# Modulation steps by single halves over all tiles, an unscaled residual stream, and a head-by-head split in a two-layer hybrid decoder

## The chip, the cores and the metric

The kernel runs on one core of a Trainium2 chip. The metric is the device time of one execution in microseconds; the median of the runs shown counts, and beside it one execution was profiled. TensorE is the matrix engine (PE in the profile), VectorE is DVE, ScalarE is ACT, GpSimd is POOL, and SyncE (SP) issues all DMA transfers.

## The reference

Two layers over 256 tokens of width 2048, float32. `shift`, `scale` and `gate` come from one conditioning vector per sequence; making them is what is called the modulation here.

```python
def hybrid_layer(x, c_act, positions, ada_w, ada_b, norm_w, w_in, ...):
    mod = c_act @ ada_w + ada_b
    shift, scale, gate = mod[:, :D_MODEL], mod[:, D_MODEL:2 * D_MODEL], mod[:, 2 * D_MODEL:]
    h = rmsnorm(x, norm_w) * (1.0 + scale[:, None, :]) + shift[:, None, :]
    u = h @ w_in
    qkv_a, beta_a, a_a, z_a, q_b, k_b, v_b, z_b, g_a, g_b = split_cols(u, SPLIT_SIZES)
    ...
    # branch A: causal conv and SiLU on q, k, v; normed q, k; gated delta rule in chunks
    o_a = gated_delta_rule(q_a, k_a, v_a, g, beta)
    o_a = rmsnorm(o_a, gdn_norm_w).reshape(b, s, GDN_WIDTH).astype(x.dtype) * jax.nn.silu(z_a)
    # branch B: rotary positions, sliding-window attention with sinks
    o_b = swa_with_sinks(q_b, k_b, v_b, sinks).reshape(b, s, SWA_WIDTH) * jax.nn.silu(z_b)
    y = jax.nn.sigmoid(g_a) * (o_a @ proj_a) + jax.nn.sigmoid(g_b) * (o_b @ proj_b)
    return x + gate[:, None, :] * (y @ w_out)
```

After both layers a final RMSNorm is applied. The modulation needs 3 x 16 column blocks of 128 in each layer, each the product of a 128x2048 block of `ada_w` with the activated conditioning vector.

## The kernel before

Everything is held transposed: 128 channels on the partitions, the 256 tokens along the row. A projection tile is one 128-column block of a weight matrix, 128x2048 floats. `load_w` (L205) fetches it as two halves of 128x1024 into the buffer `win` (five of these). `load_half` (L196) splits each half into a rounded part `whi`, cast by ScalarE (L201), and the residue `wlo`, subtracted by VectorE (L202); there are four `whi` and three `wlo` buffers. `proj` (L292) makes 16 steps of contraction, each one matmul of `whi` with 512 columns (the rounded part and the residue of the activations side by side, L289) and one of `wlo` with 256 (L290). Two PSUM banks take turns as accumulators. `evac` (L314) empties one: a copy by ScalarE (L316) and an addition by VectorE (L317), result `ub`.

The main loop (L967 to L1001) goes through the tiles of `_plan` (L46): the short ones (ba, kb, vb), then for each of two batches of eight heads qa, ka, va and, between them, the queries and gates of branch B (qb, zb); then za (the gates of branch A), pa, pb (the two output projections) and wo. Layer 0 makes the merge gates ga and gb in a group ahead of the loop; layer 1 makes eight ga tiles so and has the others within the loop, alternating with pa and pb. At a tile the loop issues the loads up to two tiles ahead, the matmuls, one step of each waiting stream (`advance`, L303), one step of the background queue (`run_bg`, L956), and then the tile's handler. The functions are traced by a framework that derives all semaphores from the tiles and sets the order on each engine from priority (program order) and readiness, so that an engine's order can depart from that of the text. On the chip each engine works through its list strictly in that order.

Three things go on beside the projections:

- *The modulation.* `ada_job` (L171) makes one column block: `ada_half` (L165) loads a 128x1024 half of `ada_w` into one of the five `win` buffers and multiplies it on VectorE with the conditioning vector, summing along the row (L168); two halves in succession, then one or two tiny operations (L177, L180). 64 such jobs are on the list (L423): the 16 gates of layer 0, then scale, shift and gate of layer 1. `ADA_RATE` (L28) gives how many jobs a tile of each kind is worth, and L993 to L996 issue a job whenever the sum reaches one. 48 must be done before layer 0's wo; the last 16 follow in layer 1's ga, pa, gb and pb tiles.
- *The preparation of branch A* (`gdn_k`, L589, and `gdn_core`, L729), a generator in the background queue, one step per tile between `yield`s: norms (`brk`, L596), a transpose on TensorE and a broadcast through DRAM (L598), decay tables, Gram matrices (L623, L624), the inversion of 32x32 triangular blocks on VectorE (L644 to L653), small DMAs that turn the blocks round (L658 to L670), matmuls that join them (T1p at L679 and following), then the chunk recurrence, whose output is `oT`. Batch 0's generator starts at va 0, batch 1's at va 8. `gdn_e` (L556) makes the decay tables `E` and `ek` of a batch when its first qa tile is handled.
- *The outputs.* `h_za` (L778) multiplies each head of `oT` with its weight and gate (L785). After every eighth za tile `split_oA` (L788) casts and subtracts two groups of four heads (L321, L322) into `oA_hl`, which pa multiplies. `split_oB` (L888) does the same for branch B at pa 2.

In wo, `h_wo` (L928) adds the gated tile to the residual (L936, L937), adds its square to the norm's sum (`norm_acc`, L358), and in layer 0 writes `x` to DRAM (L942), scales it in place by layer 1's scale (L943) and forms the two parts of `raw` (L951, L952), with which layer 1's first gates are begun before its norm is known (`group_next`, L266). `h_step` (L376) then makes layer 1's normed `h` from the scaled `x`.

## Time and profile before

| what | value |
|---|---|
| median of 3 runs | 2373.2 us (2370.95 to 2382.15) |
| the profiled execution | 2373.67 us, of which the span is 2371.9 us |
| ScalarE's share of the span | 58% |
| DMA | 531.76 MB, mean 224 GB/s |
| layer 0's loop begins, ends | 216.35, 1223.3 us |
| layer 1's loop begins | 1276.21 us |

The span runs from the first to the last instruction. A line of a group reads: line in the code, engine, operation, result <- operands, shapes, count; then busy time and the mean of one in ns; then the time that the engine stood idle in front of them, and what ended it. A line of waits reads: who <- whom, total us, times, longest. Stages are told apart by the first matmul that uses their tile.

### The profile page before, as it was taken

The numbers are of one execution on the slowest core, as the hardware profiler recorded it, in microseconds if no ns is written. First come the engines' busy times: TensorE is split into PE (matmuls) and PEld (weight loads), VectorE is DVE, ScalarE is ACT, GpSimd is POOL, SyncE is SP. The second block draws the span as 40 slices with busy tenths as digits, with TensorE's granted clock in tenths as the row PEclk, the third lists the DMA queues.
The fourth block names the chain that finished last, engine by engine and source line by source line (L and its number), as shares of the span: only waits on it lengthen the run. The fifth ranks groups of instructions, "written<-read, shape, count | busy, mean of one in ns | idle before, by whom it ended". The sixth has DMA issues, their size and how long they took to land.

```text
span 2371.9 us, 40130 instructions
## 1 busy us (share of the span) xinstructions
PE 2294.8 (97%) x15094; PEld 2026.0 (85%) x15094; DVE 1791.0 (76%) x3176; ACT 1372.8 (58%) x2621; POOL 13.9 (1%) x20
## 2 busy tenths in 40 slices
PE   7999999999999998999999999999999999999997
PEld 6999888788887887888789888888888888888886
DVE  8997888867888577788676778757786567667766
ACT  4436566667666664444445665777667755444543
POOL 0000000000000000000000000000000000000000
PEclk9999999999999999999999999999999999999999
DMA  9998675656766577998666555535555467777764
GB/s 378 360 359 277 228 243 193 194 182 203 248 202 200 164 231 257 306 316 295 216 198 198 193 179 188 184 121 193 188 172 167 135 206 267 247 243 241 252 201 143
DMA packets 185604, 531.76 MB, mean 224 GB/s; under 512 B 40449, under 2 KB 69697, under 8 KB 179905
## 3 DMA queue, kind: packets, MB, share of 16 engines
q1 hardware_dynamic: 185410, 529.20, 67.1%
q8 instruction: 118, 1.93, 0.3%
q14 instruction: 76, 0.62, 0.1%
HBM read 512.26 MB, written 16.88 MB: 223 GB/s over the span
## 4 chain that ended last, share of the span: by engine, by line
PE 76%; DVE 11%; DMA 8%; issue 3%; ACT 2%; DVEq 0%; SPq 0%; ACTq 0%
PE mm L289 39%; PE mm L290 20%; DVE wlo L202 4%; DMA adaw<-ada 4%; PE mmg L251 2%; PE mmg L250 2%; PE mmg L249 2%; DMA win<-w 2%; DMA xs_dram<-x 1%; DVE adaw L168 1%; PE o L742 1%; PE ptr L872 1%; DVE cv L526 1%; PE sc L844 1%; PE mmg L273 1%
## 5 line engine op out<-in xcount | busy, mean ns | idle before, releaser
L289 PE MATMUL mm<-h,whi 128*128 128x512 f32 x3616 | 1294.8, 398 | 18.4 <-DVE ub L317 17.3
L202 DVE TENSOR_TENSOR wlo<-win,whi 128x1024 fp32r<-128x1024 f32 x724 | 882.5, 1221 | 253.0 <-PE mm L290 142.8
L290 PE MATMUL mm<-h,wlo 128*128 128x256 f32 x3616 | 1025.7, 284 | 3.8 <-DVE wlo L202 3.8
L201 ACT CAST whi<-win 128x1024 fp32r<-128x1024 f32 x724 | 754.8, 1048 | 461.9 <-PE mm L289 248.8
L289 PEld LDWEIGHTS mm<-h,whi 128*128 128x128 f32 x3616 | 682.5, 189 | 179.8 <-issue 10.6
L290 PEld LDWEIGHTS mm<-h,wlo 128*128 128x128 f32 x3616 | 683.5, 189 | 6.4 <-DVE wlo L202 5.1
L168 DVE SCALAR_TENSOR_TENSOR adaw<-adaw,cact 128x1024 f32<-128x1024 f32 x128 | 155.9, 1222 | 71.4 <-DMA adaw<-ada 70.1
L289 PE MATMUL mm<-yhl,whi 128*128 128x512 f32 x512 | 182.9, 398 | 7.6 <-DVE x L937 4.6
L289 PE MATMUL mm<-oAhl,whi 128*128 128x512 f32 x512 | 183.7, 400 | 5.4 <-DVE oAhl L322 3.3
L289 PE MATMUL mm<-oBhl,whi 128*128 128x512 f32 x512 | 180.8, 396 | 0.5 <-DVE ub L317 0.5
L317 DVE TENSOR_TENSOR ub<-ub,mm 128x256 f32<-128x256 f32 x290 | 120.8, 417 | 63.8 <-ACT ub L316 62.7
L526 DVE SCALAR_TENSOR_TENSOR cv<-ub,par,cv 128x255 f32<-128x255 f32 (+2 forms) x288 | 138.2, 480 | 34.1 <-ACT cv L524 30.4
L290 PE MATMUL mm<-oAhl,wlo 128*128 128x256 f32 x512 | 145.6, 285 | 1.1 <-DVE wlo L202 1.1
L249 PE MATMUL mmg<-h,whi 128*128 128x256 f32 x512 | 139.1, 286 | 6.5 <-ACT h L373 6.1
L290 PE MATMUL mm<-yhl,wlo 128*128 128x256 f32 x512 | 144.9, 283 | 0.0
L290 PE MATMUL mm<-oBhl,wlo 128*128 128x256 f32 x512 | 144.0, 281 | 0.0
L250 PE MATMUL mmg<-h,whi 128*128 128x256 f32 x512 | 141.0, 283 | 0.1
L251 PE MATMUL mmg<-h,wlo 128*128 128x256 f32 x512 | 134.1, 284 | 3.2 <-DVE wlo L202 3.2
L316 ACT COPY ub<-mm 128x256 f32<-128x256 f32 x290 | 107.2, 370 | 36.6 <-PE mm L290 36.4
L289 PEld LDWEIGHTS mm<-yhl,whi 128*128 128x128 f32 x512 | 96.8, 189 | 33.1 <-issue 7.2
L289 PEld LDWEIGHTS mm<-oAhl,whi 128*128 128x128 f32 x512 | 97.6, 191 | 29.4 <-DVE oAhl L322 3.6
L289 PEld LDWEIGHTS mm<-oBhl,whi 128*128 128x128 f32 x512 | 96.2, 188 | 23.7 <-DVE ub L317 0.9
(261 smaller groups left out, 2603.5 us busy)
## 6 DMA issues: line engine op xcount, KB each, us to landing
win<-w SPq DMA_DIRECT2D x724, 512.0 KB, 4.8
adaw<-ada SPq DMA_DIRECT2D x128, 512.0 KB, 4.8
adab<-ada SPq DMA_DIRECT2D x31, 1024.0 KB, 9.1
sg<-sig_dram SPq DMA_DIRECT2D x40, 128.0 KB, 5.6
sig_dram<-gacc SPq DMA_DIRECT2D x4, 1024.0 KB, 5.6
E<-gc_dram SPq DMA_DIRECT2D x4, 1024.0 KB, 7.2
GT<-GT_d SPq DMA_DIRECT2D x4, 1024.0 KB
ob_dram<-zbs SPq DMA_DIRECT2D x32, 128.0 KB, 4.7
```

The costliest lines, as they stand in the source:

```text
L168: V.scalar_tensor_tensor(t, t, 1.0, cact[:, hf * 1024:(hf + 1) * 1024], op0=ALU.mult, op1=ALU.mult, accum_out=acc[:, hf:hf + 1])
L201: A.copy(h, w)
L202: V.tensor_tensor(o, w, h.bitcast(F32), op=ALU.subtract)
L249: T.matmul(d, hi, m[:, 0:S], start=(k == b0 and t % 2 == 0), stop=False)
L250: T.matmul(d, hi, m[:, S:2 * S], start=False, stop=False)
L251: T.matmul(d, lo, m[:, 0:S], start=False, stop=(k == b1 - 1 and t % 2 == 1))
L273: T.matmul(d, hi[:, c], m[:, 0:n], start=(k == 0), stop=False)
L289: T.matmul(ps[:, :], hi[k // 8][:, c0:c0 + P], m, start=(k == 0), stop=False)
L290: T.matmul(ps[:, S:2 * S], lo[k // 8][:, c0:c0 + P], m[:, 0:S], start=False, stop=(k == KT - 1))
L316: A.copy(t, ps[:, S:2 * S])
L317: V.tensor_tensor(t, t, ps[:, 0:S], op=ALU.add)
L526: V.scalar_tensor_tensor(y[:, j:], u[:, :S - j], w(3 - j), y[:, j:], op0=ALU.mult, op1=ALU.add)
```

## The change

Four edits go together.

1. The modulation is issued in half steps (`ada_step`): each step loads and multiplies one half; the second of a block also does the tiny operations. The list holds 128 half steps, and the sum of rates counts twice. The rates of layer 0 are new: qa and ka lower, va no longer zero, qb, zb and za higher, pa and pb lower. Layer 1's stay.
2. `x` isn't scaled in place any more. `raw` is made with the scale as an operand, and so is `h_step`'s product.
3. `split_oA` is gone. `h_za` casts and subtracts its own head right after the multiplication.
4. `gdn_k` has one empty step more after `brk` and one more before T1p.

```diff
-ADA_RATE = [dict(qa=0.45, ka=0.45, va=0.0, qb=0.275, zb=0.275, za=0.54, pa=0.54, pb=0.54), dict(ga=0.3, pa=0.3, gb=0.3, pb=0.3)]
+ADA_RATE = [dict(qa=0.25, ka=0.25, va=0.15, qb=0.45, zb=0.45, za=0.6, pa=0.45, pb=0.45), dict(ga=0.3, pa=0.3, gb=0.3, pb=0.3)]
...
-        def ada_job(l, part, ct):
-            acc = sm.tile([P, 2], F32, name="modr", tag="modr", bufs=4)
-            for hf in range(2):
-                ada_half(l, part, ct, hf, acc)
+        ada_acc = {}
+
+        def ada_step(l, part, ct, hf):
+            if hf == 0:
+                ada_acc[l, part, ct] = sm.tile([P, 2], F32, name="modr", tag="modr", bufs=4)
+            acc = ada_acc[l, part, ct]
+            ada_half(l, part, ct, hf, acc)
+            if hf == 0:
+                return
             m = modc[:, l, part, ct:ct + 1]
...
         def h_step(l, k, xa, rstd, dst):
             t = sm.tile([P, S], F32, name="hn", tag="tA", bufs=3)
-            V.tensor_tensor(t, xa, rstd, op=ALU.mult)
+            V.scalar_tensor_tensor(t, xa, modc[:, l, 1, k:k + 1], rstd, op0=ALU.mult, op1=ALU.mult)
...
+        ada_todo = [(*job, hf) for job in ada_todo for hf in range(2)]
...
                 V.tensor_tensor(brk, beta[:, :, hs], rk, op=ALU.mult)
                 yield 1
+                yield 1
                 GT = bcast_rows(brk.rearrange("p m h -> p (m h)"), "GT", "GT")
...
                 yield 1
                 yield 1
                 yield 1
+                yield 1
                 GTv = GT.rearrange("p h m t -> p (h m) t")
...
                 V.scalar_tensor_tensor(o[:, hh, :], o[:, hh, :], pr[:, PC_GNW:PC_GNW + 1], u,
                                        op0=ALU.mult, op1=ALU.mult)
-
-            def split_oA(b):
-                for j in range(2):
-                    t = big("oAhl", [P, 4, 2 * S], ("kT", "qT", "bV", "E")[2 * b + j], F32R)
-                    split_hl(t, gb_[b]["oT"][:, 4 * j:4 * j + 4, :])
-                    oA_hl[2 * b + j] = t
+                if i % 4 == 0:
+                    oA_hl[i // 4] = big("oAhl", [P, 4, 2 * S], ("kT", "qT", "bV", "E")[i // 4], F32R)
+                d = oA_hl[i // 4][:, i % 4, :]
+                A.copy(d[:, 0:S], o[:, hh, :])
+                V.tensor_tensor(d[:, S:2 * S], o[:, hh, :], d[:, 0:S].bitcast(F32), op=ALU.subtract)
...
                     dma(xs_dram[i], xo)
-                    V.tensor_scalar(xo, xo, modc[:, l + 1, 1, i:i + 1], None, op0=ALU.mult)
...
-                    A.copy(r[:, 0:S], xo)
-                    V.tensor_tensor(r[:, n:n + S], xo, r[:, 0:S].bitcast(F32), op=ALU.subtract)
+                    sc = modc[:, l + 1, 1, i:i + 1]
+                    A.activation(r[:, 0:S], xo, AF.Identity, scale=sc)
+                    V.scalar_tensor_tensor(r[:, n:n + S], xo, sc, r[:, 0:S].bitcast(F32), op0=ALU.mult, op1=ALU.subtract)
...
-                while what == "wo" and l == 0 and len(ada_todo) > KT:
-                    ada_job(*ada_todo.pop(0))
+                while what == "wo" and l == 0 and len(ada_todo) > 2 * KT:
+                    ada_step(*ada_todo.pop(0))
...
-                acc_ada += ADA_RATE[l].get(what, 0.0)
+                acc_ada += 2 * ADA_RATE[l].get(what, 0.0)
                 while ada_todo and acc_ada >= 1.0:
-                    ada_job(*ada_todo.pop(0))
+                    ada_step(*ada_todo.pop(0))
                     acc_ada -= 1.0
-                if what == "za" and i % HB == HB - 1:
-                    split_oA(i // HB)
```

## The prediction

> **What bounds the kernel now.** I read the head of the page first, then TensorE's waits.
>
> ```profile
> span 2371.9 us, 40130 instructions
> PE 2294.8 (97%) x15094; PEld 2026.0 (85%) x15094; DVE 1791.0 (76%) x3176; ACT 1372.8 (58%) x2621; POOL 13.9 (1%) x20
> ```
>
> TensorE is busy for 97% of the span, and the change gives it no matmul more or less. So only TensorE's idle time, and the time at which it runs below its full clock, can move the total. Who ends its idle time:
>
> ```profile
> PE mm L289 <- DVE ub L317: 19.4, 16, 3.1
> PE mm L290 <- DVE wlo L202: 4.9, 5, 2.2
> PE mm L289 <- DVE x L937: 4.6, 5, 1.7
> PE mm L289 <- DVE oAhl L322: 3.3, 1, 3.3
> PE nps L363 <- DVE nacc L358: 2.8, 1, 2.8
> PE GT_t L452 <- DVE brk L596: 2.1, 2, 1.1
> PE T1p L679 <- issue: 2.0, 2, 1.6
> PE T1p L679 <- DMA mt<-xdr: 1.3, 1, 1.3
> ```
>
> Columns: total us, times, longest. Nearly every wait ends on VectorE (DVE): an accumulator bank that it has not emptied (`ub`, `x`), a weight residue that it has not formed (`wlo`), the split of branch A's output. VectorE, 76% busy, is late in places.
>
> To find the places I compare the two layers. Their projection stages run the same TensorE work, but layer 1 carries no modulation step before its ga, pa, gb and pb tiles. I cut both layers at the first matmul of a stage; in each row stand the stretch, its length, and for each engine its busy time and its count of instructions. Rows 1 and 2, 3 and 4, and so on up to 11 and 12 are the same stage in layer 0 and layer 1 (qa+ka of batch 0; of batch 1; qb+zb of batch 0; of batch 1; the last eight za; the 16 tiles of pa against 16 alternating ga and pa tiles). Then come pb of layer 0 alone, the first 15 wo tiles of layer 0, and of layer 1.
>
> ```profile
> core 0: us, PE busy (x) PEld busy (x) DVE busy (x) ACT busy (x) POOL busy (x), PEclk, DMA share, GB/s
> 245.81:346.23 100.42, 95.61 (x546) 83.17 (x544) 81.97 (x140) 60.88 (x135) 0.00 (x0) 0.98 0.72 238
> 1305.65:1400.62 94.97, 93.41 (x546) 82.01 (x544) 70.64 (x112) 60.98 (x135) 0.00 (x0) 1.00 0.58 187
> 533.64:640.11 106.47, 102.47 (x622) 89.66 (x618) 84.75 (x158) 74.44 (x196) 1.81 (x1) 1.00 0.68 224
> 1577.85:1679.42 101.57, 101.56 (x622) 89.68 (x618) 72.89 (x127) 75.38 (x198) 1.81 (x1) 1.00 0.52 171
> 401.51:533.64 132.13, 125.79 (x1036) 108.80 (x1034) 99.35 (x241) 85.58 (x178) 0.52 (x1) 0.97 0.60 190
> 1454.52:1577.85 123.33, 122.01 (x1036) 106.39 (x1034) 88.83 (x219) 85.58 (x178) 0.51 (x1) 1.00 0.54 169
> 695.19:827.11 131.92, 126.12 (x1035) 108.47 (x1033) 98.69 (x241) 85.60 (x178) 0.52 (x1) 0.97 0.61 194
> 1733.32:1855.37 122.05, 122.04 (x1035) 106.31 (x1033) 86.56 (x211) 85.56 (x178) 0.52 (x1) 1.00 0.54 168
> 880.55:929.87 49.32, 45.78 (x259) 39.35 (x257) 40.09 (x63) 22.34 (x34) 0.00 (x0) 1.00 0.77 259
> 1908.80:1953.74 44.94, 44.94 (x258) 39.37 (x257) 28.98 (x34) 24.22 (x34) 0.00 (x0) 1.00 0.59 189
> 929.87:1030.64 100.77, 94.20 (x514) 81.21 (x513) 77.98 (x114) 44.36 (x56) 0.00 (x0) 0.97 0.89 301
> 1998.77:2088.69 89.92, 89.92 (x514) 78.76 (x513) 60.48 (x81) 42.46 (x57) 0.00 (x0) 1.00 0.74 247
> 1030.64:1122.28 91.64, 90.42 (x514) 78.46 (x513) 80.27 (x137) 41.67 (x62) 0.00 (x0) 1.00 0.88 299
> 1122.28:1217.47 95.19, 88.31 (x481) 75.01 (x481) 65.10 (x112) 42.66 (x65) 0.00 (x0) 0.98 0.70 222
> 2268.53:2352.90 84.37, 84.37 (x482) 73.77 (x481) 58.74 (x89) 38.16 (x47) 0.00 (x0) 1.00 0.59 184
> ```
>
> The matmul counts agree within each pair; the lengths don't. Layer 0 loses 5.45 and 4.90 us in qa+ka, 8.80 and 9.87 in qb+zb, 4.38 in the last za tiles, 10.85 in pa, 1.72 in pb (against the same 89.92 us for 16 tiles), and 10.82 in wo: 56.8 us in all. That is the pool that this change can draw on, 2.4% of the span, and layer 1 shows that the stages run without it where VectorE has room.
>
> A part of the pool is lost clock, for after some waits TensorE is granted half of its speed:
>
> ```profile
> 440.40:447.22 6.82, 6.17 (x19) 5.33 (x20) 5.53 (x14) 4.08 (x11) 0.00 (x0) 0.50 0.64 211
> 1133.30:1136.72 3.42, 3.42 (x12) 2.94 (x12) 2.34 (x4) 1.51 (x3) 0.00 (x0) 0.50 0.84 313
> ```
>
> Each such stretch costs half its length, 3.4 and 1.7 us here, on top of the wait. The waits in question are at most 3.1 us long (the `ub` row). The Trainium skill ("TensorE: Matmul & The Clock Gate", "Part 1: The HAM clock gate") says that the clock is halved after at least one idle window of some 3.4 us. By that rule no wait in the pool would halve it, and shorter waits would leave the halved stretches where they are: a forecast made by it would lie some 5 us (3.4 + 1.7) above mine. This trace has half clock behind shorter waits, so I keep the clock with the waits.
>
> **The change, part by part.** The durations that I use (busy us, mean ns of one | idle time of the engine in front of them and what ended it):
>
> ```profile
> L202 DVE TENSOR_TENSOR wlo<-win,whi 128x1024 fp32r<-128x1024 f32 x724 | 882.5, 1221 | 253.0 <-PE mm L290 142.8 <-issue 41.4 <-ACT whi L201 23.9
> L168 DVE SCALAR_TENSOR_TENSOR adaw<-adaw,cact 128x1024 f32<-128x1024 f32 x128 | 155.9, 1222 | 71.4 <-DMA adaw<-ada 70.1 <-DVE ub L317 0.2
> L322 DVE TENSOR_TENSOR oAhl<-oT,oAhl 128x1024 fp32r<-128x1024 f32 x8 | 9.8, 1220 | 0.0
> L381 DVE SCALAR_TENSOR_TENSOR h<-hn,modc,h 128x256 fp32r<-128x256 f32 x16 | 7.1, 482 | 0.3 <-ACT h L380 0.2
> L952 DVE TENSOR_TENSOR raw<-x,raw 128x256 fp32r<-128x256 f32 x16 | 6.7, 420 | 0.1
> L943 DVE TENSOR_SCALAR x<-x,modc 128x256 f32<-128x256 f32 x16 | 5.5, 347 | 29.9 <-DMA xs_dram<-x 29.9
> ```
>
> And for the modulation, VectorE's waits on its data, and the busy time of L168 alone in qa+ka, qb+zb and pb of layer 0 (two records for each half, the product and the reading of its sum):
>
> ```profile
> DVE adaw L168 <- DMA adaw<-ada: 70.1, 52, 3.3
> core 0: us, DVE busy (x), PEclk, DMA share, GB/s
> 245.81:346.23 100.42, 16.01 (x26) 0.98 0.72 238
> 401.51:533.64 132.13, 10.97 (x18) 0.97 0.60 190
> 1030.64:1122.28 91.64, 22.02 (x36) 1.00 0.88 299
> ```
>
> *x no longer scaled in place.* In wo of layer 0 every tile writes `x` to DRAM and then scales it in place at L943. The scaling must wait until the DMA has read `x`: 29.9 us with VectorE standing still, and behind it queue the next `wlo` and L936/L937, which empty the bank for TensorE. The change deletes L943 (16 x 0.347 = 5.6 us of VectorE and all 29.9 us of waiting) and turns L952, and L378 of the same size, into the three-operand form of L381: 32 x (0.482 - 0.420) = 2.0 us more VectorE, spread where it has slack (58.74 busy of 84.37 in layer 1's wo). The DMA stays, and nothing waits for it before layer 1 reads it a thousand us later. Of wo's 10.82 us, 4.6 are TensorE's waits on L937 itself; the rest is modulation still queued from pb, with the half clock at 1133.30 (1.7), and slower starts behind each wait. I take 9 off. After the last tile TensorE waits 2.8 us for the running sum of squares `nacc`, whose addition sits in the same queue: 1 off. Sum 10, bounds 5 (L937 alone) and 13.
>
> *Branch A's output split head by head.* Now two ScalarE casts and two L322 subtractions of 128x1024 follow the last za tile, and TensorE, already in pa, waits 3.3 us for one. After: each head is cast and subtracted at 128x256 directly behind its own multiplication. Behind the last head stay one cast and one subtraction of 0.42 (the L952 form). Emptying (two), gate, multiplication, cast and subtraction are six operations of 128x256 at 0.42 to 0.48, some 2.7 us in a row, and TensorE needs that head only at the last of 16 steps of the first pa tile, 15/16 of 5.62 us (89.92/16) later. So the cover is about 2.6 us (5.27 less 2.7): with a `wlo` (1.22) and a modulation half (1.22) in between it just holds, beyond that each microsecond is lost. Cost: 4 x 0.42 - 1.22 = 0.46 us of VectorE per four heads, 1.8 per layer. The Trainium skill ("VectorE: DVE Perf Modes", "The TRN2 errata") speaks against this: the fixed cost falls on every instruction, so operands should have 512 elements or more. The rows agree (0.42 is well over a quarter of 1.22), and the toll comes off slack. Taken together with pa's other loss (the split of branch B's output lies beside modulation pairs), pa gives 6 of its 10.85; bounds 2 and 9.
>
> *Modulation by halves, at new rates.* A job was two L168 in succession, 2.44 us of VectorE at one point and often a wait on DMA in front (70.1 us, 52 times); the five `win` buffers are shared with the weights, so a pair also delays two weight loads. Now one half is placed at a time. Work is unchanged in sum (96 halves before layer 0's wo), the places move, in jobs per tile: qa and ka 0.45 to 0.25, va 0 to 0.15, qb and zb 0.275 to 0.45, za 0.54 to 0.6, pa and pb 0.54 to 0.45. VectorE's demand is layer 1's busy time plus the halves. qa+ka: 70.64 + 16.01 (13 halves) = 86.7 of 94.97 us (91%) falls to 70.64 + 8 x 1.23 = 80.5 (85%). qb+zb: 88.83 + 10.97 (9 halves) = 99.8 of 123.33 (81%) rises to 88.83 + 14.4 x 1.22 = 106.4 (86%). So the load is levelled at some 85%, in steps half as long. qa+ka: 6 of 10.35 off, bounds 3 and 9. Last za tiles: the mean stays, the lumps halve, 2 of 4.38 off. pb: 0.5 of 1.72 off. qb+zb: more work in smaller lumps, which I set at nothing, between 10 gained and 25 lost; this is the largest unknown.
>
> *Two more steps in the preparation.* One empty step between `brk` and its transpose: TensorE no longer stands at the queue's head for L596, 2.1 us in two waits. One more before T1p lets the small DMAs land: 2.0 + 1.3 us of waits, some with half clock behind them. I take 2 and 4 (1 of it in layer 1), bounds 2 and 8 for both. Price: all later steps come two tiles later. Batch 0's last chunk matmuls then fall beside qa 8 and qa 9, and the `ek` buffer, which batch 1's decay tables want at qa 8, is free two tiles later; those tables are read first beside va 9 or 10, some 17 tiles on, so that hides. Batch 1 finishes beside za 5; za 8 needs it, three tiles to spare.
>
> **The sum.** The profiled execution took 2373.67 us (span 2371.9). 10 + 6 + 6 + 2 + 0.5 + 2 + 4 = 30.5 off gives 2343. The median of the runs shown, 2373.2, is the same within 0.5 us.
>
> **The rivals.**
> - *Slower: VectorE's queue in qb+zb.* VectorE works in order, and an L168 whose data have not landed holds all behind it. Now 18.7 us are lost there over 8.8 jobs, 2.1 per job. If the wait in front and not the length does the harm, every half costs what a job cost: 28.8 x 2.1 = 61 us, 42 more. Against it stand the parts that don't hang on smoothing: wo 6, pa 3, preparation 4, less load in qa+ka 5 = 18. Result 2374 + 24 = 2398. It decides from about 1.7 us per half, (18.7 + 18 + 12)/28.8. For it: 70.1 us on DMA in 52 waits, so a half waits as often as not. Against it: pb carries 18 halves in 91.64 us and loses only 1.72.
> - *No visible change: loss goes with the number of jobs.* Length doesn't matter, only the rate. qb+zb goes from 18.7 to 18.7 x 0.45/0.275 = 30.6, 12 lost against the same 18: 2374 - 6 = 2368. For it: qb+zb has the largest loss today although its mean load is the lowest of the stages with modulation.
> - *The pool empties.* Halves fit into the slack everywhere, as everything fits in layer 1, and nine tenths of 56.8 us plus 5 for the preparation go: 2374 - 56 = 2318. Against it: a load of 85% still leaves lumps.
>
> **How the numbers follow.** My forecast has 0.55, the slower rival 0.08, no visible change 0.22, the emptied pool 0.15. A difference of 0.5% (12 us) is about what a measurement of this kernel can tell from no change. The forecast's own range is 2328 to 2358, all faster; of the second rival a little lies below 2361 too. So 0.72 faster, 0.19 within, 0.09 slower. The range, 2318 to 2368, takes in the forecast, the emptied pool and the near side of the second rival.
>
> **What would show it.** The wait of VectorE on the write of `x` gone, and 15 wo tiles of layer 0 at 84 to 87 us; no TensorE wait on the split of branch A's output over 1 us; no wait on `brk`, at most 1 us at T1p; qa+ka of layer 0 within 3 us of layer 1's. The forecast is wrong if layer 0's qb+zb stretches grow past 140 us, or if the wo stretch stays near 95.

## The result, and the profile after

The changed kernel takes 2394.56 us (median of 4 runs, 2392.86 to 2399.71), the kernel before 2372.98 in runs beside them (4 runs, 2370.95 to 2382.15). The ratio is 1.0085 with a 95% interval of 1.0063 to 1.0106: slower by 0.9%, where 1.3% faster was forecast. The profiled execution took 2394.55 us, 20.9 more than that of before. Lines after L170 have moved: L202 is now L207, L289 and L290 are L294 and L295, L317 is L322, L937 is L944, the multiplication of L785 is L793, and the cast and subtraction of branch A's output are L798 and L799.

The head of the page after:

```profile
span 2392.4 us, 40175 instructions
PE 2300.3 (96%) x15094; PEld 2025.8 (85%) x15094; DVE 1790.6 (75%) x3184; ACT 1379.5 (58%) x2653; POOL 14.0 (1%) x20
```

TensorE has the same 15094 matmuls and is busy 5.5 us longer; about 2.5 of these are lost clock (the mean granted clock over the span is 0.991 before and 0.990 after). The other 15 us of the growth are idle time. VectorE has no more work than before. What has changed is what it waits for. Its group of modulation products, with the idle time in front of it, after:

```profile
L168 DVE SCALAR_TENSOR_TENSOR adaw<-adaw,cact 128x1024 f32<-128x1024 f32 x128 | 156.5, 1222 | 172.0 <-DMA adaw<-ada 171.8
```

128 products of 1.222 us, as before; but VectorE stood still 172.0 us for their data instead of 71.4. VectorE's list of waits, after, gives the number of times and the longest:

```profile
DVE adaw L168 <- DMA adaw<-ada: 171.8, 83, 4.8
DVE wlo L207 <- PE mm L295: 86.8, 101, 2.7
DVE ub L322 <- ACT ub L321: 74.9, 75, 4.9
```

The wait for the write of `x` is gone, as the prediction said. The modulation went from 52 waits and 70.1 us to 83 and 171.8, that is from 1.35 to 2.07 us for each wait. And TensorE's list, after:

```profile
PE mm L294 <- DVE ub L322: 32.4, 25, 4.0
PE mm L295 <- DVE wlo L207: 16.2, 16, 2.1
PE mm L294 <- ACT pb L873: 4.0, 1, 4.0
PE mm L294 <- DVE oAhl L799: 3.4, 1, 3.4
```

The waits on `brk` and at T1p are gone. The bank that isn't emptied went from 19.4 to 32.4 us, the missing residue from 4.9 to 16.2, and the wait on the split of branch A's output, 3.3 before, stands at 3.4.

Where the time went shows when both kernels are cut at the first matmul of each stage. The columns to the right are experiments, told below: pairs (e1: the change, but halves issued two at a time), halves alone (e5: before, with halves only), best (e15). All in us, from one profiled execution each; that of best (2350.51) was the longest of its five, whose median is 2344.02.

| stretch | before | after | pairs | halves alone | best |
|---|---|---|---|---|---|
| layer 0: qa+ka, batch 0 | 100.42 | 95.23 | 94.47 | 100.21 | 97.68 |
| qb+zb, batch 0 | 132.13 | 123.84 | 122.46 | 127.66 | 122.09 |
| qa+ka, batch 1 | 106.47 | 109.68 | 108.02 | 113.78 | 108.52 |
| qb+zb, batch 1 | 131.92 | 126.72 | 122.73 | 128.97 | 122.72 |
| za 0 to 7 | 53.44 | 63.40 | 58.76 | 53.44 | 59.79 |
| za 8 to 15 | 49.32 | 46.24 | 48.44 | 49.73 | 50.73 |
| pa | 100.77 | 99.67 | 96.79 | 99.03 | 98.47 |
| pb | 91.64 | 102.06 | 97.32 | 90.03 | 96.64 |
| wo, and on to layer 1 | 153.93 | 141.96 | 141.40 | 154.19 | 139.14 |
| layer 1: qb+zb, batch 0 | 123.32 | 122.10 | 122.36 | 123.25 | 122.31 |
| qa 8 to 15 | 54.87 | 60.06 | 60.06 | 54.88 | 54.87 |
| qb+zb, batch 1 | 122.05 | 122.20 | 122.38 | 122.00 | 122.27 |
| za 0 to 7 | 53.43 | 58.76 | 58.76 | 53.42 | 53.43 |
| ga and pa | 89.92 | 96.62 | 90.03 | 95.65 | 90.02 |
| gb and pb | 179.84 | 192.30 | 179.84 | 192.15 | 179.84 |

How far can such rows be trusted? e3, told below, changes nothing ahead of wo: there VectorE and ScalarE have the same instructions in the same order as in the kernel before. Yet its qb+zb of batch 0 takes 135.15 us against 132.13. So in layer 0 a difference of up to 3 us between two rows says nothing; in layer 1 the untouched rows of e3 agree within 0.6 us.

Layer 0 as a whole became shorter: layer 1 begins at 1265.35 instead of 1276.21 us, 10.9 earlier. Layer 1 gave back 31.4, nearly three times as much: 19.2 in its ga, pa, gb and pb tiles (6.70 + 12.46), whose rates of modulation the change leaves alone and which stood without loss before, 9.4 in the two qb+zb stretches and the eight tiles behind each, where the preparation's steps were moved, and 2.4 in the eight pa tiles ahead of ga (45.03 to 47.41), which carry halves too. The windows after, for the three worst stretches (pb of layer 0; ga and pa; gb and pb):

```profile
1021.33:1123.39 102.06, 93.76 (x512) 79.67 (x513) 78.80 (x130) 41.28 (x63) 0.00 (x0) 0.98 0.78 260
2000.16:2096.78 96.62, 92.60 (x513) 80.08 (x513) 58.55 (x80) 41.69 (x57) 0.00 (x0) 0.98 0.71 231
2096.78:2289.08 192.30, 183.37 (x1027) 157.07 (x1025) 128.87 (x188) 84.16 (x127) 0.00 (x0) 1.00 0.69 226
```

VectorE is busy 58.55 of 96.62 us in the second row, a smaller share than in any stretch of layer 0. It isn't a lack of VectorE time that stops TensorE there. VectorE's waits on its loads in this part of layer 1 (ga to the last pb), first the kernel after, then the one before:

```profile
DVE adaw L168 <- DMA adaw<-ada: 85.5, 27, 4.8
```

```profile
DVE adaw L168 <- DMA adaw<-ada: 19.1, 20, 2.8
```

Per wait that is 3.17 against 0.95 us. What such a visit looks like is to be seen in the timeline (start, length, engine, line, operation; in brackets the idle time in front). One visit in gb/pb after:

```profile
2180.00 1.22 DVE L207 TENSOR_TENSOR wlo<-win,whi 128x1024 fp32r<-128x1024 f32 x1
2181.29 0.33 SPq L167 DMA_DIRECT2D adaw<-ada  x1
...
2181.51 1.22 DVE L207 TENSOR_TENSOR wlo<-win,whi 128x1024 fp32r<-128x1024 f32 x1 [0.29 <-ACT whi L206]
2182.72 0.42 DVE L322 TENSOR_TENSOR ub<-ub,mm 128x256 f32<-128x256 f32 x1
2183.18 0.42 DVE L927 TENSOR_TENSOR ub<-ub,sg 128x256 f32<-128x256 f32 x1
2186.66 1.23 DVE L168 SCALAR_TENSOR_TENSOR adaw<-adaw,cact 128x1024 f32<-128x1024 f32 x1 [3.07 <-DMA adaw<-ada]
...
2187.82 1.22 DVE L207 TENSOR_TENSOR wlo<-win,whi 128x1024 fp32r<-128x1024 f32 x1
```

and a pair before:

```profile
2177.29 3.16 SPq L167 DMA_DIRECT2D adaw<-ada  x2
2178.87 1.23 DVE L202 TENSOR_TENSOR wlo<-win,whi 128x1024 fp32r<-128x1024 f32 x1 [1.65 <-PE mm L290]
...
2183.76 1.22 DVE L168 SCALAR_TENSOR_TENSOR adaw<-adaw,cact 128x1024 f32<-128x1024 f32 x1 [2.79 <-DMA adaw<-ada]
...
2184.91 1.22 DVE L202 TENSOR_TENSOR wlo<-win,whi 128x1024 fp32r<-128x1024 f32 x1
...
2186.39 1.22 DVE L168 SCALAR_TENSOR_TENSOR adaw<-adaw,cact 128x1024 f32<-128x1024 f32 x1
```

From issue to product it takes some 5 us in both (medians in these stages 5.4 after and 4.8 before; in the two visits shown 5.4 and 6.5). The single half is issued 2.3 us before VectorE is free for it (median in these stages, taken over the trace's records; 3.7 for the halves of pairs), so VectorE stands the rest, with the next `wlo` behind the product. In the pair shown the second half has landed by the time VectorE comes to it. Over the 13 pairs of these stages the first half waits 1.2 us on average and the second 0.3.

Why isn't the load issued sooner? It waits for a buffer. SyncE's list of waits, after:

```profile
SPq L167 <- DVE wlo L207: 138.2, 78, 9.0
```

In ga, pa, gb and pb of layer 1 each of the 27 loads goes off within 0.1 us after VectorE has finished a `wlo`, which frees a `win` buffer (above: 2181.22 and 2181.29); over the kernel 117 of the 128 go off within 0.12 us after VectorE has freed one, and 122 of 128 before. So the ring of five sets when a half's load starts, and it moves on with VectorE's own work.

### The profile page after: what moved, and what is told of

It reads as the page before. It is cut to its first block, busy times and chain, and to the rows that moved or that the text cites. A ratio compares the mean times of both kernels' runs of the same rounds, so it can differ in the third digit from the quotient of the medians.

```text
span 2392.4 us, 40175 instructions
## 1 busy us (share of the span) xinstructions
PE 2300.3 (96%) x15094; PEld 2025.8 (85%) x15094; DVE 1790.6 (75%) x3184; ACT 1379.5 (58%) x2653; POOL 14.0 (1%) x20
## 2 busy tenths in 40 slices
DMA packets 185604, 531.76 MB, mean 222 GB/s; under 512 B 40449, under 2 KB 69697, under 8 KB 179905
## 4 chain that ended last, share of the span: by engine, by line
PE 64%; DMA 15%; DVE 14%; issue 4%; ACT 3%; SPq 0%; DVEq 0%; ACTq 0%
PE mm L294 32%; PE mm L295 16%; DMA adaw<-ada 11%; DVE wlo L207 6%; PE mmg L256 2%; PE mmg L255 2%; PE mmg L254 2%; DVE LX L656 1%; DMA win<-w 1%; DVE mt L654 1%; DVE adaw L168 1%; DMA sg<-sig_dram 1%; ACT whi L206 1%; DVE ub L322 1%; PE sc L851 1%
## 5 line engine op out<-in xcount | busy, mean ns | idle before, releaser
L294 PE MATMUL mm<-h,whi 128*128 128x512 f32 x3616 | 1295.7, 399 | 28.6 <-DVE ub L322 21.8
L207 DVE TENSOR_TENSOR wlo<-win,whi 128x1024 fp32r<-128x1024 f32 x724 | 880.8, 1220 | 208.5 <-PE mm L295 86.8
L295 PE MATMUL mm<-h,wlo 128*128 128x256 f32 x3616 | 1025.4, 284 | 5.8 <-DVE wlo L207 5.8
L294 PEld LDWEIGHTS mm<-h,whi 128*128 128x128 f32 x3616 | 682.4, 189 | 194.4 <-DVE ub L322 22.9
L295 PEld LDWEIGHTS mm<-h,wlo 128*128 128x128 f32 x3616 | 683.5, 189 | 9.3 <-DVE wlo L207 8.9
L168 DVE SCALAR_TENSOR_TENSOR adaw<-adaw,cact 128x1024 f32<-128x1024 f32 x128 | 156.5, 1222 | 172.0 <-DMA adaw<-ada 171.8
L294 PE MATMUL mm<-oAhl,whi 128*128 128x512 f32 x512 | 183.2, 398 | 8.7 <-DVE ub L322 5.2
L294 PE MATMUL mm<-oBhl,whi 128*128 128x512 f32 x512 | 183.6, 399 | 5.5 <-DVE ub L322 5.4
L294 PE MATMUL mm<-yhl,whi 128*128 128x512 f32 x512 | 181.8, 397 | 2.6 <-DVE yhl L933 2.6
L322 DVE TENSOR_TENSOR ub<-ub,mm 128x256 f32<-128x256 f32 x290 | 120.7, 416 | 75.7 <-ACT ub L321 74.9
L295 PE MATMUL mm<-oBhl,wlo 128*128 128x256 f32 x512 | 145.4, 284 | 8.8 <-DVE wlo L207 8.8
L295 PE MATMUL mm<-oAhl,wlo 128*128 128x256 f32 x512 | 145.3, 284 | 1.7 <-DVE wlo L207 1.7
L295 PE MATMUL mm<-yhl,wlo 128*128 128x256 f32 x512 | 145.1, 283 | 0.0
L294 PEld LDWEIGHTS mm<-oAhl,whi 128*128 128x128 f32 x512 | 97.1, 190 | 33.0 <-DVE ub L322 4.4
L294 PEld LDWEIGHTS mm<-oBhl,whi 128*128 128x128 f32 x512 | 96.9, 189 | 30.3 <-DVE ub L322 8.1
L294 PEld LDWEIGHTS mm<-yhl,whi 128*128 128x128 f32 x512 | 96.9, 189 | 25.8 <-DVE yhl L933 2.9
```

The source lines that it names most:

```text
L168: V.scalar_tensor_tensor(t, t, 1.0, cact[:, hf * 1024:(hf + 1) * 1024], op0=ALU.mult, op1=ALU.mult, accum_out=acc[:, hf:hf + 1])
L207: V.tensor_tensor(o, w, h.bitcast(F32), op=ALU.subtract)
L294: T.matmul(ps[:, :], hi[k // 8][:, c0:c0 + P], m, start=(k == 0), stop=False)
L295: T.matmul(ps[:, S:2 * S], lo[k // 8][:, c0:c0 + P], m[:, 0:S], start=False, stop=(k == KT - 1))
L322: V.tensor_tensor(t, t, ps[:, 0:S], op=ALU.add)
```

## The experiments

Medians against the kernel before on the same chip. Runs that share a median of before were made together.

| run | what | median, before beside it (us) | ratio (95%) |
|---|---|---|---|
| e1 | after, halves in pairs | 2356.43, 2376.57 | 0.991 (0.9895 to 0.9925) |
| e2 | after, without the two steps | 2391.92, 2376.57 | 1.0057 (1.0036 to 1.0079) |
| e8 | after, halves not loaded | 2335.12, 2376.57 | 0.9819 (0.9803 to 0.9836) |
| e9 | after, load one step ahead | 2395.91, 2376.57 | 1.0075 (1.0053 to 1.0097) |
| e10 | after, product held to the next tile | 2380.74, 2377.23 | 1.0012 (0.9997 to 1.0028) |
| e3 | before, `x` unscaled | 2360.79, 2377.23 | 0.9925 (0.990 to 0.995) |
| e4 | before, head-by-head split | 2376.26, 2377.23 | 0.9999 (0.9982 to 1.0017) |
| e5 | before, halves | 2389.13, 2377.23 | 1.0054 (1.0034 to 1.0073) |
| e6 | before, new rates | 2369.88, 2378.97 | 0.996 (0.9941 to 0.9979) |
| e13 | before, the two steps | 2381.63, 2378.97 | 1.0009 (0.9997 to 1.0022) |
| e1_old_steps | e1 without the two steps | 2357.63, 2378.97 | 0.9914 (0.9887 to 0.9941) |
| e1_old_t1p | e1 without T1p's step | 2363.07, 2378.97 | 0.9935 (0.9912 to 0.9958) |
| e14 | e13, one copy moved to VectorE | 2367.98, 2372.53 | 0.9981 (0.9967 to 0.9994) |
| e15 | e1, the steps in layer 0 only | 2344.02, 2372.53 | 0.988 (0.986 to 0.990) |

### e1: are the single halves the cause?

```diff
-                acc_ada += 2 * ADA_RATE[l].get(what, 0.0)
+                acc_ada += ADA_RATE[l].get(what, 0.0)
                 while ada_todo and acc_ada >= 1.0:
                     ada_step(*ada_todo.pop(0))
+                    ada_step(*ada_todo.pop(0))
```

> The changed kernel, only with the two halves of a block issued together again (rates, unscaled x, head split and extra steps as changed). Theory (each visit of VectorE to a modulation half stands and waits for that half's data, and single halves double the visits): VectorE's wait on the modulation data falls from 171.8 us to about 75, layer 1's ga/pa and gb/pb stretches return from 96.6 and 192.3 us to about 90 and 180, the time to 2360-2376 us. Rival (the new rates, more modulation in qb, zb and za, are what costs): 2388-2396 us, layer 1's stretches unchanged.

Everything else stays, and the time falls from 0.9% above the kernel before to 0.9% below it. VectorE's wait on the loads and the windows of ga/pa and gb/pb, e1:

```profile
DVE adaw L168 <- DMA adaw<-ada: 82.9, 63, 4.2
```

```profile
1981.57:2071.60 90.03, 90.03 (x512) 78.88 (x513) 60.61 (x81) 42.47 (x57) 0.00 (x0) 1.00 0.75 247
2071.60:2251.44 179.84, 179.84 (x1027) 157.30 (x1025) 130.85 (x191) 87.07 (x127) 0.00 (x0) 1.00 0.75 246
```

The wait is halved, and layer 1's stretches are back at the times of before with TensorE busy throughout. Of the 38 us between the two profiled executions some 20 lie in layer 1 and 19 in layer 0 (za 4.6 less 2.2, pb 4.7, qb+zb 5.4, pa 2.9, qa+ka 2.4, the rest small); single terms of layer 0 are hardly above the scatter of 3 us, their sum is.

### e2: without the two steps

```diff
                 V.tensor_tensor(brk, beta[:, :, hs], rk, op=ALU.mult)
                 yield 1
-                yield 1
...
                 yield 1
-                yield 1
                 GTv = GT.rearrange("p h m t -> p (h m) t")
```

> The changed kernel without the two extra steps of the preparation. Theory (the moved T1p matmuls had covered the softmax queue on ScalarE; without them TensorE waits 4 us and drops to half clock in each of four qb+zb stretches): 10 to 13 us back, 2381-2385 us, layer 1's stretches from qb to the next ka at 178 and 175 us instead of 182 and 181. Rival (the steps are worth their gain and the loss in those stretches comes from elsewhere): 2396-2402 us, with the T1p and brk waits back.

1.0057 against the change's 1.0085, with intervals that overlap: at most a small gain. In layer 1 qb+zb with the eight tiles behind it falls from 182.16 to 177.47 us (122.10 + 60.06 to 122.59 + 54.88) and from 180.96 to 175.64 (122.20 + 58.76 to 122.21 + 53.43); in layer 0 qb+zb rises, from 123.84 to 128.62 and from 126.72 to 135.76. But layer 0 as a whole takes 1048.0 us with the steps and 1048.5 without (from its loop's first matmul to that of layer 1), for the tiles behind qb+zb are longer with them (za 0 to 7: 63.40 against 54.88). e13 shows the steps without the halves.

### e8: the halves' products without their loads

```diff
-            dma(t, ada_d[l, part, ct, :, hf * 1024:(hf + 1) * 1024])
-            V.scalar_tensor_tensor(t, t, 1.0, cact[:, hf * 1024:(hf + 1) * 1024], ...
+            V.scalar_tensor_tensor(t, cact[:, hf * 1024:(hf + 1) * 1024], 1.0, cact[:, hf * 1024:(hf + 1) * 1024], ...
```

> The changed kernel with the load of each half in the loop left out: VectorE multiplies the conditioning vector with itself into the same buffer of the ring, so its work, the order and the use of the ring stay, and only the waiting for data goes (the modulation values are then not the reference's). Theory (the wait costs): 2340-2360 us, layer 1's ga/pa and gb/pb stretches at 90 and 180. Rival (VectorE's time for halves in the wrong places, or the ring's slots, cost): over 2385 us.

The product and the buffer are still there, only the load (and with it the wait) is not. 2335.12, 59 us under the change. ga/pa takes 89.92, gb/pb 179.84, and pb of layer 0 is at its floor of 16 tiles (window, e8):

```profile
997.65:1087.68 90.03, 90.03 (x514) 78.57 (x513) 80.11 (x129) 42.84 (x65) 0.00 (x0) 1.00 0.64 208
```

VectorE is busier in this window (80.11 of 90.03) than in the one after (78.80 of 102.06), and nothing is lost. So the product's own time costs nothing here; its data cost it all. e8 also takes 67 MB of transfers away (531.76 to 464.62), so it doesn't tell the wait from the traffic; e10 does.

### e9: the load one step earlier in the text

```diff
+            t = ada_ready.pop(0)
+            if ada_todo:
+                ada_load(*ada_todo[0])
```

> The changed kernel with each half loaded one step before it is multiplied; the buffer comes from the same ring of five. Theory (the wait for data costs, and a lead of one step ends it): VectorE's wait on modulation data under 40 us, 2350-2370 us. Rival (the ring is what is short: a half that is held for a step takes a fifth of the weights' buffers, and weights come late instead): 2390 us or more, with ScalarE's and VectorE's waits on weights up.

No gain, 2395.91. VectorE's wait on the loads, e9:

```profile
DVE adaw L178 <- DMA adaw<-ada: 166.0, 77, 5.2
```

The time from issue until VectorE is free for the product, the lead, is still 2.3 us in layer 1's stages. Each half has its load a whole step earlier in the text, but it still goes off only when a buffer comes free (26 of 26 in these stages within 0.1 us after a `wlo`), and the order on the engines is the framework's own. Moving the load in the text doesn't move the product away from its landing, so the theory of a lead wasn't tested here. The rival isn't borne out either: ScalarE's wait for weights fell, from 105.6 to 84.5 us.

### e10: the product tied to a later tile

```diff
-            V.scalar_tensor_tensor(t, t, 1.0, cact[:, hf * 1024:(hf + 1) * 1024], ...
+            tok = ...   V.tensor_scalar(tok, last_ub[0][:, 0:1], 0.0, 1.0, op0=ALU.mult, op1=ALU.add)
+            V.scalar_tensor_tensor(t, t, tok, cact[:, hf * 1024:(hf + 1) * 1024], ...
```

> The changed kernel with single halves, but the product of a half is tied to the next tile: its factor 1.0 is made by a tiny VectorE operation from that tile's ub, so that VectorE can't come to the product earlier than one tile after the load was issued, whatever order the framework would choose. The buffer stays in the ring of five and is held longer, and 128 tiny operations of about 0.27 us come on top (34 us of VectorE). Theory (a single half is reached 2.3 us after its load is issued, and the load needs about 5): VectorE's wait on modulation data under 35 us, 2345-2365 us. Rival (what is short is the ring, so that any load in it delays weights): 2380 us or more, with waits on weights up.

The factor 1.0 is made out of the next tile's `ub`, so the product can't be placed ahead of it. Now no wait on a modulation load is left in VectorE's list, and the lead is 12 us. Layer 1's ga/pa and gb/pb with all loads in place, and pb of layer 0 (windows, e10):

```profile
1031.47:1130.92 99.45, 93.81 (x515) 78.31 (x513) 80.97 (x140) 43.31 (x63) 0.00 (x0) 1.00 0.80 259
2008.18:2098.10 89.92, 89.92 (x515) 78.77 (x513) 64.77 (x95) 43.05 (x58) 0.00 (x0) 1.00 0.77 247
2098.10:2277.94 179.84, 179.84 (x1027) 157.25 (x1025) 135.16 (x205) 88.01 (x127) 0.00 (x0) 1.00 0.74 243
```

The two rows of layer 1 are at the times of before, and DMA's busy share in ga and pa is above that after (0.77 against 0.71): with the wait gone, the traffic costs nothing there. This settles ga, pa, gb and pb of layer 1. Layer 0 it doesn't settle. Its pb gains only 2.6 of 10.4, and as a whole it takes 1056.1 us, 8 more than in the change, with no wait on modulation data left; the total of 2380.74 lies in the rival's range. ScalarE's wait for weights doubles, as the rival said (first e10, where the cast is L220, then after):

```profile
ACT whi L220 <- DMA win<-w: 214.2, 148, 4.8
```

```profile
ACT whi L206 <- DMA win<-w: 105.6, 71, 5.5
```

A half that waits a tile for its product holds one of the five `win` buffers that the weights need. That this is what keeps layer 0 long isn't shown: in pb ScalarE's wait for weights is 31.6 us, but in the kernel before, whose pb takes 91.64, it is 30.3. e10 also gives VectorE 124 tiny operations more (18.6 us).

### e3, e4, e5, e6: each of the other parts alone, on the kernel before

e3 takes edit 2 of the change alone, e4 edit 3, e5 the half steps at the old rates, e6 the new rates with pairs. One line of each, in this order:

```diff
-                    V.tensor_scalar(xo, xo, modc[:, l + 1, 1, i:i + 1], None, op0=ALU.mult)
...
-                    split_oA(i // HB)
...
+        ada_todo = [(*job, hf) for job in ada_todo for hf in range(2)]
...
-ADA_RATE = [dict(qa=0.45, ka=0.45, va=0.0, qb=0.275, zb=0.275, za=0.54, pa=0.54, pb=0.54), dict(ga=0.3, pa=0.3, gb=0.3, pb=0.3)]
+ADA_RATE = [dict(qa=0.25, ka=0.25, va=0.15, qb=0.45, zb=0.45, za=0.6, pa=0.45, pb=0.45), dict(ga=0.3, pa=0.3, gb=0.3, pb=0.3)]
```

> The kernel before, only with x no longer scaled in place. Theory: the 10 us forecast for this part, nearly all in the 15 wo tiles of layer 0 (95.2 to 85-87 us): 2364-2368 us. Rival (the gain comes out only beside the other edits, since VectorE is late there from the modulation in pb): under 4 us, over 2372.

> The kernel before, only with branch A's output split head by head. By the forecast's step TensorE's wait on the split (3.3 us) goes, and pa gains 5: 2370-2372 us. Theory after the changed kernel's profile (TensorE still waits 3.4 us there, for the last head's split lies behind wlo and modulation on VectorE as the batch split did): no gain, 2375-2381 us.

> The kernel before, only with the modulation by single halves, at the old rates. Theory: the wait on modulation data goes from 70 to 170 us or more, layer 1's ga/pa and gb/pb stretches to about 96 and 192 us as in the changed kernel, layer 0's pb over 100, in all 25 to 45 us slower: 2400-2420 us. Rival (halves are harmful only with the new rates or beside the head-by-head split): under 2385 us.

> The kernel before, only with the new rates of layer 0, blocks still made by pairs. By the forecast's step (levelled load) qa+ka of layer 0 get some 6 us shorter and qb+zb stay as they are: 2368-2374 us. Rival (qb+zb lose in proportion to the jobs moved there, 12 us, and pa and pb don't gain): 2378-2386 us.

- e3: 16.4 us off the median; in its profile 12.2 in the wo stretch (153.93 to 141.70), and no wait on the write of `x`. The profiled execution was the longest of the four (2370.55): ahead of wo it is 8 us longer than that of before, in stretches that e3 leaves as they were.
- e4: no difference, as its theory said and not the forecast. The wait on the split (L791 there) is still 3.8 us.
- e5: 11.9 us slower, where 25 to 45 was expected. ga/pa 95.65 and gb/pb 192.15, as in the change; so the loss there belongs to the halves alone. Its pb of layer 0 stays at 90.03, though, where over 100 was expected.
- e6: 9.1 us faster. qa+ka of batch 0 falls from 100.42 to 93.92, below layer 1's 94.97; qb+zb of batch 0 goes to 129.37 and that of batch 1 rises to 140.73, 6 us more for both; the prediction had bounded the price of more work there at 25. The profiled execution took 2375.70, above the median of 2369.88.

VectorE's wait on loads, and the two windows of layer 1, e5:

```profile
DVE adaw L168 <- DMA adaw<-ada: 132.1, 62, 5.1
```

```profile
1994.45:2090.09 95.64, 91.19 (x514) 78.77 (x513) 56.85 (x77) 41.81 (x57) 0.00 (x0) 1.00 0.70 228
2090.09:2282.24 192.15, 183.49 (x1026) 158.63 (x1025) 127.85 (x186) 84.57 (x128) 0.00 (x0) 0.99 0.67 224
```

Without the halves the parts add up: e3, e4, e6 and e13 give -16.4 - 1.0 - 9.1 + 2.7 = -23.8 us, and all four together (e1) give -20.1. With them they don't: the halves cost 12 alone and some 40 in company (0.991 to 1.0085). The difference lies in layer 0, which in e5 is 4 us shorter than before and in the change 19 longer than in e1. In pb the median lead is 7.0 us in e5 (1.08 halves a tile, nearly the rhythm of the tiles) and 3.9 in the change (0.9 a tile). That the lead differs is seen; why loads and products come to stand so at one rate and not at the other was not found out.

### e13, e14: where the two steps lose what they win

e13 is the kernel before with one `yield` more behind `brk` and one more before T1p (edit 4). e14 is e13 and, for the qb tiles only:

```diff
-            A.copy(t, ps[:, S:2 * S])
+            (V.tensor_copy if on_vector else A.copy)(t, ps[:, S:2 * S])
```

> The kernel before, only with the two extra steps of the preparation. Theory (in layer 1 the softmax queue on ScalarE comes uncovered twice, a 4 us wait and half clock each): layer 1 10 us longer, seen in its qa of batch 1 and za stretches at 60.1 and 58.8 us with qb+zb no shorter; layer 0 between 5 shorter and 5 longer: 2381-2392 us. Forecast's step: 5 us faster, 2370-2373 us.

> The kernel before with the two extra steps, and with the first copy that empties a qb tile's bank made by VectorE and not by ScalarE (32 copies of 128x256, some 0.4 us each, move over). Theory (with the steps moved, TensorE's next tile waits for a qb bank whose ScalarE copy stands behind the softmax): the 4 us waits on ub in layer 1's qb+zb vanish and those two stretches get 4 to 6 us shorter each than the 123.6 and 122.4 us with the steps alone, the rest of the layer as with the steps. Rival (another cause, VectorE's own queue, sets those waits): the two stretches stay within 2 us.

e13: no difference, 1.0009. In its profile layer 0 is 7.6 us shorter and layer 1 11.6 longer. Layer 0's qb+zb falls from 132.13 and 131.92 to 124.49 and 122.85, and the tiles that T1p's matmuls move to grow by 5.2 and 5.3 (qa 8 to 15: 63.16, za 0 to 7: 58.76). In layer 1 those grow alike (54.87 to 60.10, 53.43 to 58.76), but qb+zb doesn't shrink: 123.62 and 122.43. A wait has taken T1p's place there (TensorE's list for the first of these stretches, e13):

```profile
PE mm L289 <- DVE ub L317: 4.8, 2, 4.1
```

What it waits for is a bank copy on ScalarE that stands behind the softmax of branch B. The same place in the kernel after, where TensorE stands idle from 1507.15 to 1511.19 (ScalarE's timeline):

```profile
1509.65 0.38 ACT L872 ACTIVATE pb<-pb,ls 128x128 f32<-128x128 f32 x1
1509.94 0.49 ACT L873 ACTIVATE pb<-pb,ls 128x256 f32<-128x256 f32 x1
1510.34 0.35 ACT L321 COPY ub<-mm 128x256 f32<-128x256 f32 x1
```

In the kernel before T1p's 62 matmuls (1514.50 to 1515.69) and the work around them fell into this tile and covered ScalarE's queue: with the steps taken out again (e1_old_steps, below) TensorE's waits on `ub` from layer 1's qa to its pa come to 1.3 us. e14 tests it by giving the qb banks' copy to VectorE: the 4 us wait goes (the longest left in these stretches is 1.4), the first stretch shrinks from 123.62 to this (window, e14), the second from 122.43 to 119.34:

```profile
1441.35:1561.29 119.94, 117.22 (x987) 101.01 (x985) 89.15 (x221) 79.82 (x162) 1.61 (x3) 1.00 0.54 173
```

3.7 and 3.1 us in these places, a little under the 4 to 6 expected, and a ratio that falls from 1.0009 to 0.9981.

### e1_old_t1p, e1_old_steps, e15: which step, and in which layer

All three start from e1. e1_old_t1p takes the new `yield` before T1p out, e1_old_steps both new ones, and e15 does this to both:

```diff
-                yield 1
+                if l == 0:
+                    yield 1
```

> The changed kernel with pairs and without the extra step ahead of T1p alone; the one after brk stays. Theory (T1p beside the softmax is what matters): like the kernel without both steps or up to 2 us faster, 2341-2349 us. Rival (any shift of the steps by one tile uncovers it, the one after brk too): 2352-2358 us, the 4 us wait in layer 1's qb+zb still there or at another tile.

> The changed kernel with pairs and without the two extra steps. Theory (the steps cost 10.5 us in layer 1 and nothing in layer 0): 2343-2349 us against 2356 with them. Rival (layer 0 loses without them what layer 1 gains, as the single-half kernel without the steps was only 2.6 us faster): 2353-2359 us.

> The changed kernel with pairs, and with the two extra steps in layer 0 alone. Theory (pairs, unscaled x, rates and steps add up; the steps gain some 10 us in layer 0 and lose 10 in layer 1): 2344-2349 us, the fastest so far, layer 1's stretches as before the change. Rival (layer 0's gain with the steps was chance of one order): 2354-2359 us, like the kernels with both or neither.

With the step behind `brk` alone (e1_old_t1p) layer 1's qb+zb takes 127.35 and 126.98, though the tiles behind it are back near their old length (qa 8 to 15: 56.39): TensorE waits for `ub` up to 3.9 us there, so shifting the preparation by one tile already uncovers ScalarE's queue. Its 2363.07 us is above both ranges expected. Without both (e1_old_steps) layer 1 is as before (122.52, 122.32; qa 8 to 15 54.91, za 53.43), and layer 0's qb+zb goes back up to 129.12 and 136.56: 2357.63, no better than e1. With the steps in layer 0 only (e15) both stay low, and this is the fastest of the kernels that make the whole modulation, 2344.02 us, within the range expected and 0.988 (0.986 to 0.990) of the time before.

## Why the prediction was wrong, point by point

**The step that failed** is the one on the modulation by halves. It took the length of a visit for the harm ("in steps half as long") and the sum of VectorE's load for the measure ("the load is levelled at some 85%"). The runs show that the wait in front of a visit does the harm: VectorE does its list in order (in the visit shown the next `wlo` starts only at 2187.82, behind the product), a load is issued when VectorE frees a buffer, shortly before its product's turn comes, and there are more waits, each longer (83 of 2.07 us over the kernel, 52 of 1.35 before). In layer 1's ga, pa, gb and pb this is shown: e5 (halves alone) has the loss, and e1 (pairs), e8 (no load) and e10 (no wait) don't. In layer 0 e1 shows that the halves cost 19 us beside the other edits; that there too it is the wait, and not the ring of buffers, stays open, for e10 took the wait away and layer 0 got no shorter. The forecast also missed the place: layer 1's rates stay, but its visits double. Layer 1's ga, pa, gb and pb had no term in the sum; they cost 19.2 us.

- *x not scaled in place.* Right in its mechanism. Forecast 10 off, 12.0 measured in the stretch (12.2 in e3; e3's median says 16.4, with an interval of 12 to 24). The first 15 wo tiles came to 88.80 where 84 to 87 was named; a stretch of 3.4 us at half clock, behind a wait of 2.6 for the last pb tile's split, is still in them.
- *Head-by-head split, and pa.* Forecast 6 off; pa gave 1.1, less than the scatter, and e4 shows no gain. The cover of 2.6 us was reckoned with one `wlo` and one modulation half in between, each at its own length. VectorE's timeline at the last head, after (pa begins at 921.66):

```profile
925.28 1.23 DVE L168 SCALAR_TENSOR_TENSOR adaw<-adaw,cact 128x1024 f32<-128x1024 f32 x1 [2.15 <-DMA adaw<-ada]
...
927.90 0.41 DVE L322 TENSOR_TENSOR ub<-ub,mm 128x256 f32<-128x256 f32 x1
...
928.80 0.48 DVE L793 SCALAR_TENSOR_TENSOR oT<-oT,par,ub 128x256 f32<-128x256 f32 x1 [0.30 <-ACT ub L791]
929.21 1.22 DVE L207 TENSOR_TENSOR wlo<-win,whi 128x1024 fp32r<-128x1024 f32 x1
931.03 1.23 DVE L168 SCALAR_TENSOR_TENSOR adaw<-adaw,cact 128x1024 f32<-128x1024 f32 x1 [0.61 <-DMA adaw<-ada]
...
932.18 0.42 DVE L799 TENSOR_TENSOR oAhl<-oT,oAhl 128x256 fp32r<-128x256 f32 x1
```

  The last za tile's bank is emptied only at 927.90, 6.2 us after pa began, behind a half that waited 2.15; then a second half stands, wait included, between the multiplication and the subtraction. TensorE waits 3.44 us, until 932.66. From the start of pa to the end of the last head's split it takes 10.9 us, where the prediction had 2.7 for the chain and a cover of 5.27.
- *qa+ka, last za.* Forecast 6 and 2 off. qa+ka of batch 0 gave 5.2 and came within 0.3 us of layer 1's, as named; e6 shows that the rates do this without halves. qa+ka of batch 1 grew by 3.2, but T1p's 5.2 moved into it. The last za tiles gave 3.1. Both of these are about the scatter. za 0 to 7, which had no term, grew by 10.0, of which 5.3 is T1p's work (e13).
- *qb+zb.* Set at nothing between 10 gained and 25 lost; 8.3 and 5.2 off, mostly because T1p's work moved out (the steps alone, e13, take 7.6 and 9.1 off). The mark of 140 us was not reached, nor did wo stay near 95: neither of the two signs that the prediction named for its being wrong showed.
- *pb of layer 0.* Forecast 0.5 off, 10.4 on.
- *Two more steps.* Forecast 6 off, 1 of it in layer 1; e13 measures none. The waits named did go (`brk`, T1p), and layer 0 gained 7.6 in e13's profile. That T1p's tile was also cover for ScalarE's softmax in layer 1 was not looked at: the step was priced by whom it releases, and not by what it had hidden.

The sum: 30.5 off was forecast, 20.5 on came in the profiled execution's span. Of these 51 us, layer 1 makes 32.4 (1 off forecast, 31.4 on) and layer 0 18.6 (29.5 off forecast, 10.9 off), over half of it pb.

**The rivals.** The slower one, with 0.08, had the mechanism and nearly the time (2398), but the time by luck. Its place was wrong: qb+zb, the only stretch where it was looked for, got shorter. Its price of 2.1 us per half is a stage's loss per job, and is not borne out by VectorE's 2.07 us per wait, which is another quantity; in layer 1's ga, pa, gb and pb 19.2 us were lost over 27 halves, 0.7 each. Its evidence against, that pb carried 18 halves for a loss of 1.72, was evidence about pairs: they came two at a time, and VectorE waited there three times, 5.2 us in all; with halves it waits 13 times, 21.1 us. No visible change, with 0.22, took the rate alone to count; 12 us more in qb+zb were its price, and e6, which changes the rates alone, has 6 there and is faster as a whole. The emptied pool (2318) is what e8 comes near to, without loads.

**Open.** Why single halves spoil layer 0's pb at 0.9 a tile and not at 1.08 is not settled, nor what costs layer 0 its 19 us, the wait or the buffers. Since the loads wait for a buffer, a ring of their own for the halves is the next thing to try; it wasn't run.

## What to carry to other kernels

Splitting background work into smaller pieces on an engine that works in order adds places at which it can wait for data: compare the load's time from issue to landing with the time that is left until the product's turn comes, before comparing lengths. Look also at what the load's issue waits for: here it was a buffer, so an earlier place in the text changed nothing. A rate that stays unchanged is still a change if the unit behind it is halved, so go through every stage that uses it. And before moving a step to rid it of a wait, look at what else that step's time was hiding, in every layer that runs it.

## What the runs showed of the hardware

TensorE can be granted half clock after waits of about 2 us, but isn't always. In ga/pa of the kernel after, a wait of 2.09 us for `wlo` ends at 2029.17; the clock a little later (windows, after):

```profile
2030.00:2031.00 1.00, 1.00 (x4) 0.86 (x4) 0.97 (x3) 0.00 (x0) 0.00 (x0) 0.50 1.02 258
2031.00:2032.00 1.00, 1.00 (x5) 0.84 (x4) 1.00 (x2) 0.00 (x0) 0.00 (x0) 0.50 0.88 287
```

A longer wait, of 2.56 us for `ub` (867.14 to 869.70), left the clock whole (window, after):

```profile
867.00:876.00 9.00, 6.44 (x37) 5.53 (x36) 8.03 (x14) 4.20 (x9) 0.00 (x0) 1.00 0.65 213
```

What tells the two apart isn't shown. In gb/pb TensorE waits 8.8 us in eight waits of at most 2.1, and its busy time for the same matmuls grows by 3.5 (179.84 to 183.37); the granted clock is 1.00 there, so that isn't lost clock, and what it is was not found out. The Trainium skill ("TensorE: Matmul & The Clock Gate", "Part 1: The HAM clock gate") gives an idle window of some 3.4 us as the condition; the half clock behind 2.09 us differs, and the rows decide.
